# One block of convolution and recurrence: four banks for the first DFT stage, other steps for recurrence, filter network and final preparation

## The chip, the cores and the metric

The kernel runs on one core of one Trainium2 chip. The core has a matrix engine (TensorE, PE in the profile; PEld is its weight load), a vector engine (VectorE, DVE), a scalar engine (ScalarE, ACT), a general engine (GpSimd, POOL), and SyncE (SP), which here only issues DMAs. The metric is device time in microseconds (us) of one execution; lower is better. A matmul's result goes to PSUM, which has eight banks of 128 x 512 fp32 values; DVE or ACT must read a bank ("evacuate" it) before PE writes it again.

## What is computed

A block for 4096 latent tokens and 256 context tokens of 1024 values: a modulated RMS norm, one input projection, a gated long convolution (Hyena) on one part of the columns, a recurrence in both directions (RG-LRU) on the other, and one output projection onto the residual.

```python
def hyena_filter(L, f_w1, ..., f_freq):          # 2L x 512, from a small network
    z = jnp.concatenate([t, jnp.cos(f * w), -jnp.sin(f * w)], axis=-1)
    h = jnp.sin(fr[0] * (z @ f_w1 + f_b1))
    h = jnp.sin(fr[1] * (h @ f_w2 + f_b2))
    h = jnp.sin(fr[2] * (h @ f_w3 + f_b3))
    h = (h @ f_w4) * jnp.exp(-t * deltas[None, :])
    ...
def long_conv(u, kernel, bias):
    uf = jnp.fft.rfft(u, n=2 * L, axis=1)
    kf = jnp.fft.rfft(kernel, n=2 * L, axis=0)
    y = jnp.fft.irfft(uf * kf[None], n=2 * L, axis=1)[:, :L]
    return y + u * bias
def rglru_bidir(xr, ...):                        # gates a, b from two small products
    xc = dwconv(xr, conv_w, (2, 1)) + conv_b
    hf = linear_scan(a_f, b_f, h0_f, False)      # h = a * h + b along the tokens
    hb = linear_scan(a_b, b_b, h0_b, True)       # the same from the last token back
def mixer_out(p, y_rnn, kernel, ...):
    u = dwconv(p[..., :3 * D_HYENA], hy_conv_w, (1, 1)) + hy_conv_b
    x0, x1, v = jnp.split(u, 3, axis=-1)
    y_h = long_conv(v * x1, kernel, hy_bias) * x0
    y = jnp.concatenate([rms_norm(y_h, gn_h) * silu(z_h), rms_norm(y_rnn, gn_r) * silu(z_r)], axis=-1)
    return y @ w_out
```

## The kernel before

Every fp32 product of the two projections is made of three fp16 products (high by high, high by low, low by high), so an output tile of 128 x 512 takes 24 matmuls. The long convolution is a DFT of 8192 points split into 128 x 64, in fp16 pairs too. The program has these stages; the times are those of the profiled execution.

- **Start (0 to 62 us).** The modulation products `mod` (tile `wm` streams in), the first four token tiles are loaded and normed (`xsplit`, L454: scale on DVE; L456: high fp16 half on ACT; L458: low half on POOL; L459/L460: two DMA transposes on SP into `X`), and the weights of the `xr` columns are prepared (tile `wh`).
- **Pass A (62 to about 850 us).** Eight chunks of 512 tokens, twelve steps each; a step is one output tile of `xr`, `x1` or `v` (24 matmuls `mm<-X,wh`). Side work is hung on a step list: `at(d, f)` calls `f` d steps later, `tick()` runs what is due. The side work of the first chunk or two is the weights, the context (`ctx_in` at step CT = 5, 7, 9; its gates are `fa<-xc,gw` and ACT L788), and the filter network `mlp`: three layers by four pieces of 512 positions, a matmul pair (a fp32 matmul is two instructions) into `fa` or `fb`, one ACT pass, five DVE passes (L850 to L854: `q`, `q`, `x`, `x`, `x`) and a sine on ACT (L855) each. At step FS = 10 `filt` begins the filter itself: 16 groups of rows (`filter_group`), a new one about every FD = 4.95 steps.
- **Pass B (about 850 to 1790 us).** Chunks 7 to 0, twelve steps each (`zr`, `x0`, `zh`). The backward recurrence `units_b` is a generator of seven phases: loads; gates; their exponentials; square root; scan with the product into `zr` and its sum of squares; `yscale`, which puts that sum through PE (`p2b_yr`, a matmul into `sm`) to find a scale; the scaled fp16 halves to DRAM. The steps at which chunks 7 to 1 advance it are in DS; chunk 0 has its own (D0).
- Beside pass B `fft_gen` advances, 1.75 pulls a step: the first DFT stage of u (`s1u_gen`, 64 groups, about 925 to 1222 us), then the per-slot work, then the inverse.
- **Phase out (about 1852 to 2241 us).** 32 output tiles of 128 tokens, four per chunk: `ohalf` with `wz,hl` (24 matmuls x 2) for the convolution's half, and with `X,hl` for the recurrence's, seven to eight tiles ahead. `oprep` prepares the next chunk's `hl` in three parts, called after the tiles OP1, OP2 and OP3 of a chunk; the third part writes `hl` (L1430 on ACT, L1431 on DVE).

A scheduler sorts each engine's instructions by priority, which the code's order gives; matmuls made with `mms` rank 64 places lower. PSUM is shared by all: `mm` 3 banks, `fa` 2, `fb` 2, `sm` 1. One group of the first DFT stage is

```python
vo = pool.tile([128, 4, 2, 128], F16, name="vo", bufs=2)
ps = self.pst("fa", 2)
self.mms(ps, st1[:, 0:128], rhs, True, False)
self.mms(ps, st1[:, 128:256], rhs, False, True)
nc.scalar.activation(vo[:, :, 0, :], pv, AF.Copy)             # L1160
nc.vector.tensor_sub(vo[:, :, 1, :], pv, vo[:, :, 0, :])      # L1161
nc.sync.dma_start(self.VuD[:, j, n0:n0 + 4, :], ...)          # L1163
```

and four groups share one transposed input `ut`, which comes from `ua` (L1148 ACT, L1149 DVE) by a DMA transpose.

Of the kernel before, what the change touches and what calls it, by code (L numbers as in the profile page):

```python
# [10 lines left out]
F32 = mybir.dt.float32  # L11
F16 = mybir.dt.float16
# [10 lines left out]
D = 1024  # L23
# [6 lines left out]
CT = 5  # L30
ML = 1
MK = 1
FS = 10
RQ = 1
OD = 7
OP1 = (0, 0)
RL = 8
IZ = 3
OP2 = 1
OP3 = 2  # L40
PW = ()
IA = (1, 1)
FL = (2, 3)
# [4 lines left out]
MS = ()  # L48
XS = ((1, 1, 2), (1, 2, 3))
PB = {"mm": 3, "fa": 2, "fb": 2, "sm": 1}  # L50
FD = 4.95
XK = ((6, 9), (0, 4))
NX = 11
D0 = (8, 11, 12, 13, 14, 16, 17, 17)
WO = (9, 13, 16)
SEQ = [(2, "zr"), (2, "x0"), (1, "x0"), (1, "zr"), (0, "x0"), (0, "zh"), (0, "zr"), (2, "zh"), (1, "zh")]
XL = [(6, "zr"), (5, "zr"), (4, "zr"), (3, "zr"), (2, "zr"), (1, "x0"), (0, "x0"), (2, "zh")]
DS = (1, 4, 7, 7, 9, 9, 10)
DA = ((12, 14, 15, 15), (4, 4, 6, 6), (3, 5, 6, 8))
EPS = 1e-6  # L60
MAGIC = 1.5 * 2.0 ** 23
# [102 lines left out]
class K:  # L164
# [420 lines left out]
    def pass_a(self):  # L585
        tc, nc, a = self.tc, self.nc, self.a
        with ExitStack() as es, ExitStack() as right:
# [9 lines left out]
            ml = ml_.__enter__()  # L597
            sp_ = tc.tile_pool(name="start", bufs=1)
            sp = sp_.__enter__()
            if True:  # L600
                self.columns(sp)
                self.tap_sums()
                m = self.mod(sp, ml, ap, 1)
                next(m)
                self.cpos = ap.tile([128, 512], F32, name="cpos")
                for h in range(2):
                    nc.scalar.dma_start(self.cpos[64 * h:64 * h + 64], a["t_pos"])
                xt = [hy.tile([128, 1028], F32, name="xc", bufs=4)[:, :D] for k in range(3)]
                xr = [self.xload(ap, tok(0), 0, xt[:2], xt[2].rearrange("p (k c) -> p k c", k=2)),
                      self.xload(ap, tok(2), 2)]  # L610
                raw = self.xp_.tile([128, NB, 8, 128], F32, name="X", bufs=2)
                for j in range(NB):
                    nc.sync.dma_start(raw[:, j], a["w_in"][COLS["xr"] + j])
                self.pull(m)
                m = self.mod(sp, ml, ap, 0)
                next(m)
                for k in range(2):
                    self.xsplit(ap, xr[k], self.s1, self.sx, dst(X, 2 * k))
                gs = [self.wprep("xr", j, raw[:, j]) for j in range(NB)]
                for k in range(2):  # L620
                    for j, g in enumerate(gs):
                        W["xr", j] = next(g)
                self.pull(m)
                for g in gs:
                    next(g)

            def wpair(k):
                raw = sp.tile([128, 2, 8, 128], F32, name="wm", bufs=4)
# [13 lines left out]
            def filt():  # L642
# [4 lines left out]
                next(g)  # L647
                for d in FL:
                    self.at(d, lambda: next(g))
            mlp = self.mlp(ml)  # L650
            for k in range(4):
                self.at(k, lambda k=k: wpair(NB + 2 * k))
            self.at(3, recur)
# [2 lines left out]
            ctx = self.ctx_in(ap, hy, W)  # L656
            for d in (0, 2, 4):
                self.at(CT + d, lambda: next(ctx))
            for k in range(10):
                self.at(ML + k // MK, lambda: self.pull(mlp, 1))  # L660
            self.at(FS, filt)
            for n in range(16):
                self.at(FS + FG + int(FD * n), lambda n=n: self.filter_group(self.flt, n))
# [165 lines left out]

    def mlp(self, pool):  # L830
        nc, a = self.nc, self.a
        ws = pool.tile([128, D], F32, name="bm", bufs=1)[:, :384].rearrange("p (l c) -> p l c", l=3)
        nc.scalar.dma_start(ws, a["f_w"])
        fc = pool.tile([128, 6], F32, name="fc")
        nc.vector.tensor_mul(fc[:, 0:3], self.col[:, 104:107], self.col[:, 107:110])
# [299 lines left out]
    def s1u_gen(self, pool, st1):  # L1135

        nc = self.nc
        for j in range(NB):
            u = pool.tile([128, T], F32, name="u", bufs=1)
            for h in range(2):  # L1140
                nc.sync.dma_start(u[:, 2048 * h:2048 * h + 2048], self.uD[j][:, 2048 * h:2048 * h + 2048])
            tot = self.cp.tile([128, 1], F32, name=f"ut{j}")
            nc.vector.tensor_reduce(tot, self.usq[:, j], axis=AX.X, op=OP.add)
            s, self.su[j] = self.pow2(self.cp, tot, 9, 0, f"u{j}", 1)
            uv = u.rearrange("c (m n) -> c n m", n=64)
            for q in range(4):
                ua = pool.tile([128, 16, 2, 64], F16, name="ua", bufs=1)
                nc.scalar.activation(ua[:, :, 0, :], uv[:, 16 * q:16 * q + 16, :], AF.Copy, scale=s)  # L1148
                nc.vector.scalar_tensor_tensor(ua[:, :, 1, :], uv[:, 16 * q:16 * q + 16, :], s, ua[:, :, 0, :],  # L1149
                                               op0=OP.mult, op1=OP.subtract)  # L1150
                ut = pool.tile([128, 16, 128], F16, name="ut", bufs=2)
                nc.sync.dma_start_transpose(ut, ua.rearrange("c n h m -> c (n h m)"))
                for g in range(4):
                    vo = pool.tile([128, 4, 2, 128], F16, name="vo", bufs=2)
                    ps = self.pst("fa", 2)
                    rhs = ut[:, 4 * g:4 * g + 4, :]
                    self.mms(ps, st1[:, 0:128], rhs, True, False)
                    self.mms(ps, st1[:, 128:256], rhs, False, True)
                    pv = ps.rearrange("p (n c) -> p n c", c=128)
                    nc.scalar.activation(vo[:, :, 0, :], pv, AF.Copy)  # L1160
                    nc.vector.tensor_sub(vo[:, :, 1, :], pv, vo[:, :, 0, :])  # L1161
                    n0 = 16 * q + 4 * g
                    nc.sync.dma_start(self.VuD[:, j, n0:n0 + 4, :], vo.rearrange("p n h c -> p n (h c)"))  # L1163
                    yield
# [356 lines left out]
```

## Time and profile before

| what | value |
|---|---|
| median of 3 runs | 2239.83 us (2232.47 to 2243.2) |
| profiled execution | 2242.97 us |
| its span in the trace | 2241.2 us |
| PE busy | 1934.0 us, 86% of the span |
| DVE, ACT, POOL busy | 1362.1, 1173.0, 623.2 us |
| mean granted clock of PE | 0.943 of full speed |

The profiled execution lies 3.1 us above the median, inside the range of the runs, and 1.8 us above its span. PE has the largest busy share in every stage; what it idles is 2241.2 - 1934.0 = 307 us. A row of a timeline gives in brackets how long the engine was idle before it and whose work ended that.

### The profile page before, as it was taken

To read this page: it belongs to the slowest core of one execution; us is meant where nothing else is said; L and a number is where in the kernel's file an instruction comes from. 1 tells how busy PE (TensorE), PEld (TensorE's weight loads), DVE (VectorE), ACT (ScalarE), POOL (GpSimd) and SP (SyncE) were. 2 spreads that over 40 slices of the span, in tenths; PEclk is the share of its full clock that TensorE was granted. 3 is DMA by queue.
4 is the path that set the end of the run, shared out by engine and by line. 5 is a ranking of instruction groups with operands and counts; after the bars stand their busy time and mean duration, and the time that the engine had idled before them with its cause. 6 is when DMAs were issued, how large, how long until landed. Compare 5 with 4: busy or idle time off the path is not lost. (4 is left out here: it accounts for less than half of the span.)

```text
span 2241.2 us, 30015 instructions
## 1 busy us (share of the span) xinstructions
PE 1934.0 (86%) x10640; PEld 933.0 (42%) x10640; DVE 1362.1 (61%) x2629; ACT 1173.0 (52%) x1828; POOL 623.2 (28%) x417
## 2 busy tenths in 40 slices
PE   6866989989889899878888989898898858999997
PEld 2443434434334344333334545454443434444443
DVE  3894676756647567564543663744745565766576
ACT  2655766664656578576573733744556531432232
POOL 3024344343424321111211342533423300111130
PEclk9987989999999999989999999999999879999999
DMA  9547354565544522666746889889998798344332
GB/s 286 196 123 209 102 184 136 179 171 150 191 126 129 141 90 84 204 184 196 219 147 212 200 202 253 216 217 232 236 234 229 186 264 234 112 143 150 115 125 104
DMA packets 397028, 398.43 MB, mean 178 GB/s; under 512 B 208809, under 2 KB 295359, under 8 KB 392270
## 3 DMA queue, kind: packets, MB, share of 16 engines
q1 hardware_dynamic: 381020, 356.93, 56.4%
q10 hardware_dynamic: 15858, 39.59, 6.0%
q8 instruction: 84, 1.38, 0.3%
q14 instruction: 66, 0.54, 0.1%
HBM read 206.62 MB, written 146.81 MB: 158 GB/s over the span
## 5 line engine op out<-in xcount | busy, mean ns | idle before, releaser
L169 PE MATMUL mm<-X,wh 128*128 128x512 f16 x3072 | 733.4, 386 | 32.2 <-DVE cvx L536 10.2
L169 PEld LDWEIGHTS <-wh 128*128 128x128 f16 x3648 | 325.8, 100 | 455.5 <-issue 93.4
L169 PE MATMUL mm<-X,wz 128*128 128x512 f16 x1536 | 371.9, 389 | 9.8 <-ACT zh L1023 5.0
L169 PEld LDWEIGHTS <-wz 128*128 128x128 f16 x1728 | 158.2, 100 | 226.7 <-issue 58.8
L169 PEld LDWEIGHTS <-hl 128*128 128x128 f16 x1536 | 149.7, 99 | 222.7 <-issue 37.8
L169 PE MATMUL mm<-wz,hl 128*128 128x512 f16 x768 | 176.7, 385 | 18.4 <-DVE oxt L1445 6.9
L169 PE MATMUL mm<-X,hl 128*128 128x512 f16 x768 | 174.7, 382 | 9.5 <-DMA hl<-hlD 9.5
L463 POOL TENSOR_TENSOR acc<-acc,dec 128x512 f32<-128x512 f32 x64 | 88.1, 1377 | 237.2 <-ACT dec L941 227.7
L463 POOL TENSOR_TENSOR oacc<-oacc,osq 128x512 f32<-128x512 f32 x21 | 38.5, 1833 | 330.9 <-ACT oacc L1417 327.8
L466 POOL TENSOR_TENSOR I<-I,xc 128x1024 f32<-128x1024 f32 (+3 forms) x36 | 84.4, 2348 | 161.4 <-ACT I L788 155.0
L169 PE MATMUL fa<-xc,gw 128*128 128x512 f32 (+3 forms) x152 | 79.2, 614 | 46.2 <-DVE cvv L531 19.4
L1201 POOL TENSOR_TENSOR A<-A,B 128x256 f32<-128x256 f32 x64 | 53.1, 829 | 229.1 <-DVE B L1200 194.9
L458 POOL TENSOR_TENSOR xlo<-xt,xh 128x1024 f16<-128x1024 f32 x32 | 74.3, 2344 | 140.1 <-ACT xh L456 140.1
L169 PE MATMUL fb<-tb,vki 128*128 128x128 f16 x768 | 98.2, 225 | 14.6 <-DMA tb<-in_t_s 9.8
L169 PE MATMUL fa<-tb,vu 128*128 128x128 f16 x768 | 97.7, 225 | 0.0
L812 DVE TENSOR_TENSOR_SCAN I<-R,car,I 128x512 f32<-128x512 f32 (+2 forms) x64 | 97.2, 1540 | 0.1
L1212 DVE SCALAR_TENSOR_TENSOR yy<-A,yy 128x512 f16<-128x512 f32 x64 | 56.6, 885 | 64.6 <-ACT yy L1211 64.5
L1199 DVE TENSOR_TENSOR A<-fa,kf 128x512 f32<-128x512 f32 x64 | 43.9, 686 | 81.0 <-ACT kf L1195 78.1
L169 PEld LDWEIGHTS <-vki 128*128 128x128 f16 x768 | 77.2, 101 | 29.5 <-issue 17.9
L466 POOL TENSOR_TENSOR zr<-zr,sg 128x1024 f32<-128x1024 f32 x16 | 39.5, 2466 | 175.7 <-ACT sg L1069 140.9
L169 PE MATMUL fb<-xc,gw 128*128 128x512 f32 (+3 forms) x152 | 77.8, 601 | 10.2 <-ACT I L788 5.0
L463 POOL TENSOR_TENSOR hf<-hf,I 128x1024 f32<-128x1024 f32 x16 | 50.0, 3127 | 129.1 <-DVE I L812 82.2
(345 smaller groups left out, 3420.8 us busy)
## 6 DMA issues: line engine op xcount, KB each, us to landing
VkD<-vk SPq DMA_DIRECT2D x64, 256.0 KB, 2.4
VuD<-vo SPq DMA_DIRECT2D x64, 256.0 KB, 2.6
X<-XD SPq DMA_DIRECT2D x8, 2048.0 KB, 9.6
vu<-VuD SPq DMA_DIRECT2D x128, 128.0 KB, 3.7
vki<-VkD SPq DMA_DIRECT2D x128, 128.0 KB, 3.3
ZD<-zo SPq DMA_DIRECT2D x64, 256.0 KB, 3.5
xt<-in_x SPq DMA_DIRECT2D x30, 512.0 KB, 5.0
xpD<-xt SPq DMA_DIRECT2D x28, 512.0 KB, 3.7
```

The source lines that it names most:

```text
L169: self.nc.tensor.matmul(out, lhsT, rhs, start=start, stop=stop)
L458: nc.gpsimd.tensor_sub(xl, xt, xh)
L463: self.nc.gpsimd.tensor_add(out, x, y)
L466: self.nc.gpsimd.tensor_mul(out, x, y)
L812: nc.vector.tensor_tensor_scan(f(h), f(r), f(h), 0.0 if c is None else c, op0=OP.mult, op1=OP.add)
L1199: nc.vector.tensor_mul(A, u4, kf[:, :, 0:1, :].to_broadcast([128, NB, 2, 64]))
L1201: nc.gpsimd.tensor_sub(A[:, :, 0, :], A[:, :, 0, :], B[:, :, 1, :])
L1212: nc.vector.scalar_tensor_tensor(yy[:, :, 1, :], yv, 0.125, yy[:, :, 0, :], op0=OP.mult, op1=OP.subtract)
```

## The change

There are four edits. The first DFT stage of u takes its PSUM banks in turn from `fb` and `fa` (four in all, where it had the two `fa`), with four output tiles `vo` and two input tiles `ua`. The steps DS of the backward recurrence become (1, 4, 6, 7, 8, 10, 11): exponentials and scan a step earlier, the scale and the fp16 halves a step or two later. OP2 and OP3 become 0 and 1, so the second and third part of `oprep` are called one output tile earlier. The filter network leaves the step list: it has a weight tile of its own, its first part is called in the start behind the weight loads, five more parts behind the second modulation's first part, and the rest at the end of the start; `filt` comes at step 5, its groups every 5.2 steps.

```diff
-FS = 10
+FS = 5
...
-OP2 = 1
-OP3 = 2
+OP2 = 0
+OP3 = 1
...
-FD = 4.95
+FD = 5.2
...
-DS = (1, 4, 7, 7, 9, 9, 10)
+DS = (1, 4, 6, 7, 8, 10, 11)
...
                 for j in range(NB):
                     nc.sync.dma_start(raw[:, j], a["w_in"][COLS["xr"] + j])
+                mlp = self.mlp(ml)
+                self.pull(mlp, 1)
                 self.pull(m)
                 m = self.mod(sp, ml, ap, 0)
                 next(m)
+                self.pull(mlp, 5)
                 for k in range(2):
                     self.xsplit(ap, xr[k], self.s1, self.sx, dst(X, 2 * k))
...
                 for g in gs:
                     next(g)
+                self.pull(mlp)
...
-            mlp = self.mlp(ml)
...
-            for k in range(10):
-                self.at(ML + k // MK, lambda: self.pull(mlp, 1))
...
-        ws = pool.tile([128, D], F32, name="bm", bufs=1)[:, :384].rearrange("p (l c) -> p l c", l=3)
+        ws = pool.tile([128, 3, 128], F32, name="ws")
...
-                ua = pool.tile([128, 16, 2, 64], F16, name="ua", bufs=1)
+                ua = pool.tile([128, 16, 2, 64], F16, name="ua", bufs=2)
...
-                    vo = pool.tile([128, 4, 2, 128], F16, name="vo", bufs=2)
-                    ps = self.pst("fa", 2)
+                    vo = pool.tile([128, 4, 2, 128], F16, name="vo", bufs=4)
+                    ps = self.pst("fa" if g % 2 else "fb", 2)
```

How the order of instructions moves is shown at three places. First DVE in the start, where the first four token tiles are scaled (`xc` and `xt`, L454). Before:

```order
L315 SCALAR_TENSOR_TENSOR rq_x<-rt_x,rq_x 128x2 x2
L295 TENSOR_SCALAR sw<-col,es 128x4
L454 SCALAR_TENSOR_TENSOR xc<-xc,rq_x,s_149 128x1024 x2
L454 SCALAR_TENSOR_TENSOR xt<-xt,rq_x,s_149 128x1024 x2
L489 SCALAR_TENSOR_TENSOR wh<-X,p2s_w,wh 128x1024
```

After the change (`q` and `x` are the filter network's tiles):

```order
L454 SCALAR_TENSOR_TENSOR xc<-xc,rq_x,s_149 128x1024
L851 TENSOR_SCALAR q<-x 128x512 x2
L852 TENSOR_SCALAR q<-q 128x512 x2
L853 SCALAR_TENSOR_TENSOR x<-q,x 128x512 x2
L854 SCALAR_TENSOR_TENSOR x<-q,x 128x512 x2
L855 TENSOR_SCALAR x<-x 128x512 x2
L454 SCALAR_TENSOR_TENSOR xc<-xc,rq_x,s_149 128x1024
L315 SCALAR_TENSOR_TENSOR rq_x<-rt_x,rq_x 128x2
L358 TENSOR_TENSOR mr<-mm,bm 2x256
L454 SCALAR_TENSOR_TENSOR xt<-xt,rq_x,s_149 128x1024
L863 TENSOR_TENSOR q<-x,q 128x512
L454 SCALAR_TENSOR_TENSOR xt<-xt,rq_x,s_149 128x1024
```

Ten passes of the filter network now stand between the first two scalings, and twenty more stand ahead of the first; eight of its twelve matmul pairs stand ahead of the first matmul of `X` on PE. On SP six loads of `w_in` now stand ahead of the last pair of transposes of `X`, two of them ahead of the first pair and three more ahead of the second; before it was one, ahead of the third pair.

The second place is PE at the first groups of the first DFT stage of u (`st1u` are its constants, `ut` its input). Before:

```order
L169 LDWEIGHTS st1u
L169 MATMUL fa<-ut,st1u 128x512
L169 LDWEIGHTS st1u
L169 MATMUL fa<-ut,st1u 128x512
L169 LDWEIGHTS st1u
L169 MATMUL fa<-ut,st1u 128x512
L169 LDWEIGHTS st1u
L169 MATMUL fa<-ut,st1u 128x512
L169 LDWEIGHTS wh
L169 MATMUL mm<-X,wh 128x512
```

After:

```order
L169 LDWEIGHTS st1u
L169 MATMUL fb<-ut,st1u 128x512
L169 LDWEIGHTS st1u
L169 MATMUL fb<-ut,st1u 128x512
L169 LDWEIGHTS st1u
L169 MATMUL fa<-ut,st1u 128x512
L169 LDWEIGHTS st1u
L169 MATMUL fa<-ut,st1u 128x512
L169 LDWEIGHTS st1u
L169 MATMUL fb<-ut,st1u 128x512
```

Where two groups stood together ahead of the projection's matmuls, four now do, in four banks.

The third place is DVE at the end of chunk 7's backward recurrence (`q1r` and `p2b_yr` lead to the scale's matmul on PE). Before:

```order
L1087 TENSOR_TENSOR zr<-zr,hf 128x1024
L1161 TENSOR_TENSOR vo<-fa,vo 128x4x128
L814 COPY car_8311<-I 128x1
L1087 TENSOR_TENSOR zr<-zr,hf 128x1024
L1149 SCALAR_TENSOR_TENSOR ua<-u,p2s_u_8373,ua 128x16x64
L1111 TENSOR_REDUCE q1r<-qs 128x1
L190 CAST p2b_yr<-q1r 128x1
```

After:

```order
L1088 TENSOR_TENSOR zr<-zr,hf 128x1024
L815 COPY car_8276<-I 128x1
L1088 TENSOR_TENSOR zr<-zr,hf 128x1024
L1162 TENSOR_TENSOR vo<-fb,vo 128x4x128
L1162 TENSOR_TENSOR vo<-fa,vo 128x4x128
L1150 SCALAR_TENSOR_TENSOR ua<-u,p2s_u_8341,ua 128x16x64 x2
L1112 TENSOR_REDUCE q1r<-qs 128x1
L190 CAST p2b_yr<-q1r 128x1
```

One more `ua` pass and two `vo` passes stand ahead of `p2b_yr`. On PE the number of projection matmuls (`mm`) between the chunk's last gate matmul and the `p2b_yr` matmul goes, for chunks 7, 6, 5, 4, 3, 2, 1, 0, from 73, 107, 100, 121, 70, 66, 85, 90 to 103, 127, 127, 152, 74, 67, 89, 101.

## Rows read from the trace of the kernel before

**Rows 1.** Page part 1: busy time, share of the span, instructions.

```profile
PE 1934.0 (86%) x10640; PEld 933.0 (42%) x10640; DVE 1362.1 (61%) x2629; ACT 1173.0 (52%) x1828; POOL 623.2 (28%) x417
```

**Rows 2.** Windows: us, busy time per engine (instructions), PE clock, DMA share, GB/s.

```profile
0.00:62.00 62.00, 38.54 (x148) 13.86 (x149) 26.93 (x93) 20.56 (x30) 20.62 (x16) 0.89 1.00 281
...
118.00:213.00 95.00, 60.20 (x359) 36.71 (x358) 63.28 (x168) 48.84 (x96) 32.98 (x20) 0.83 0.60 144
213.00:850.00 637.00, 577.04 (x2407) 253.15 (x2408) 423.68 (x771) 403.68 (x678) 243.51 (x149) 0.96 0.48 149
850.00:1240.00 390.00, 339.16 (x1699) 154.91 (x1698) 204.38 (x364) 242.47 (x331) 76.42 (x35) 0.95 0.59 179
...
1880.00:2241.20 361.20, 326.93 (x1684) 151.69 (x1681) 230.87 (x488) 100.38 (x155) 48.45 (x29) 0.98 0.39 127
```

**Rows 3.** Waits, 118 to 213 us: total, times, longest.

```profile
PE mm L169 <- DMA X<-xh: 8.9, 1, 8.9
...
PE mm L169 <- DVE xc L536: 7.1, 1, 7.1
...
PE fa L169 <- ACT R L788: 6.5, 1, 6.5
...
PE fb L169 <- ACT x L855: 4.4, 2, 2.3
ACT L788 <- DMA dec<-in_f_w: 4.0, 1, 4.0
```

**Rows 4.** Timeline of PE in pass A: start, length, count, idle before it.

```profile
83.63 1.02 PE L169 MATMUL fb<-x,bm 66*128 66x512 f32 x2
...
123.72 10.52 PE L169 MATMUL mm<-X,wz 128*128 128x512 f16 x48
```

**Rows 5.** Timeline of DVE at the start.

```profile
42.29 4.35 DVE L454 SCALAR_TENSOR_TENSOR xt<-xt,rq_x,s 128x1024 f32<-128x1024 f32 x2
```

**Rows 6.** Tile x on DVE (MLP): ns min/median/max, first and last start.

```profile
L850 DVE TENSOR_SCALAR q<-x x12: 410/418/427, 85.5 to 157.8; 128x512 f32<-128x512 f32 x12
...
L853 DVE SCALAR_TENSOR_TENSOR x<-q,x x12: 681/683/2487, 88.8 to 160.6; 128x512 f32<-128x512 f32 x12
```

**Rows 7.** Timeline of POOL, 130 to 142 us.

```profile
134.89 6.42 POOL L458 TENSOR_TENSOR xlo<-xt,xh 128x1024 f16<-128x1024 f32 x2 [76.14 <-ACT xh L456]
```

**Rows 8.** Timeline of DVE, 130 to 142 us.

```profile
136.84 2.49 DVE L853 SCALAR_TENSOR_TENSOR x<-q,x 128x512 f32<-128x512 f32 x1
```

**Rows 9.** Timeline of SP's DMA queue at the start.

```profile
56.70 1.79 SPq L460 DMA_TRANSPOSE X<-xlo  x1
```

**Rows 10.** Waits, 850 to 1240 us.

```profile
DVE vo L1161 <- ACT vo L1160: 49.6, 22, 7.7
...
ACT vo L1160 <- DMA VuD<-vo: 23.0, 10, 5.5
...
PE fa L169 <- DVE vo L1161: 21.3, 12, 5.3
...
PE sm L169 <- DVE p2b_yr L190: 7.1, 1, 7.1
```

**Rows 11.** Tile vo: ns min/median/max, first and last start.

```profile
L1160 ACT ACTIVATE vo<-fa x64: 572/590/630, 936.7 to 1220.8; 128x512 f16<-128x512 f32 x64
L1161 DVE TENSOR_TENSOR vo<-fa,vo x64: 664/690/705, 938.9 to 1221.5; 128x512 f16<-128x512 f32 x64
```

**Rows 12.** Waits, whole span.

```profile
PE sm L169 <- DVE p2b_yr L190: 28.8, 5, 9.4
```

**Rows 13.** Waits, 1880 to 2241 us.

```profile
PE mm L169 <- DVE oxt L1445: 6.9, 4, 2.0
...
PE mm L169 <- DVE hl L1431: 4.7, 8, 0.7
...
PE mm L169 <- ACT hl L1430: 3.3, 2, 1.8
```

**Rows 14.** Timeline of PE in the middle of pass A.

```profile
566.60 2.08 PE L169 MATMUL fa<-xc,gw 128*128 128x512 f32 x2 [8.33 <-DVE cvv L531]
```

## The prediction

> **What bounds the kernel now.** I read the page's busy times first: PE works 1934.0 of 2241.2 us, DVE 1362.1, the others less [rows 1]. So only PE's idle time, 307 us, can be won unless PE's own work or its clock changes; the edits add no matmul. The windows say where that idle time lies: 23.5 us of the first 62 (62.00 - 38.54), 34.8 of the 95 from 118 to 213, 60 of the 637 of pass A after that, 51 of the 390 in which the first DFT stage of u runs, 34 of the last 361 [rows 2]. The start is not held by an engine: its DMA share is 1.00. From 118 to 213 us PE is idle for more than a third of the time and its granted clock is 0.83, against 0.96 in the next window [rows 2]; that is the stretch of the filter network and the context.
>
> Then I read, stage by stage, which wait of PE ends last. From 118 to 213 us: 4.4 us for the network's sine, 7.1 for `xc`, 6.5 for the context's first gate, 8.9 for the next `X` behind it [rows 3]. In the first DFT stage: 21.3 us in 12 waits for `vo`, and 7.1 for chunk 7's `p2b_yr` [rows 10]. Over the span `p2b_yr` costs 28.8 us in five waits, the longest, 9.4, in chunk 0 [rows 12]. In phase out: 4.7 us for DVE's `hl`, 3.3 for ACT's, 6.9 for the evacuation into `oxt` [rows 13]. These names are the ones that the edits touch, and they sum to some 92 us. In pass A's middle there are stalls of about 8 us, of which one is shown [rows 14]; they end on DVE's convolution passes, which wait for ACT, and the filter's rows share ACT and POOL with them.
>
> The durations are those of the profiled execution, 2242.97 us (span 2241.2, 1.8 around it), 3.1 above the median of 2239.83. The sum is made against 2242.97.
>
> **Start and filter network.** The network is twelve pieces. One takes a pair of matmul instructions, 1.02 us [rows 4], and five DVE passes: three of 0.42 and two of 0.68 (the short ones taken alike), 2.62 us [rows 6]. Nothing is removed; it is moved.
>
> Gain: eight of the twelve pairs come to stand ahead of the first `X` matmul, where PE is idle anyway. 8 x 1.02 is 8.2; since the record's end includes the pipeline I take 0.86 a pair, -7. The waits of 4.4 for the sine go for those eight, but four pieces remain in chunk 0: -3.
>
> Cost: 30 DVE passes, six pieces, stand ahead of the fourth `xt` scaling: 6 x 2.62 = 15.7, and with one more pass about 16.4 us, if all were in line. DVE is busy only 26.93 us of the first 62 [rows 2], and 20 of the 30 passes stand ahead of the first scaling, in that idle time; ten stand between the first two. The first two scalings take 4.35 us a pair in these rows [rows 5], two passes of about 2.2. I take a delay of 5 us for the first `X` matmuls: the ten passes are 5.2. The ends are 0 (all in idle time) and 16.4.
>
> One row speaks against putting DVE's passes beside POOL: the pass that takes 0.68 in the median took 2.49 at 136.84 us [rows 6, 8], within POOL's two subtractions, 6.42 us from 134.89 [rows 7]. POOL is busy 20.62 us in the first 62 [rows 2]. If each of its microseconds held DVE up, the ten or thirty passes would be late by up to 20.6; by the rows, one such meeting costs 1.8 us. My 5 us includes that two or three of the passes meet no POOL work. The Trainium skill, "SBUF — State Buffer", section "SBUF: two separate sides", says that DVE and GpSimd share a port pair as an exclusive lock, so that a DVE operation with two SBUF inputs and a GpSimd operation that reads SBUF shut each other out for a whole instruction. The trace agrees in that one case of 2.49 us; by the rule the start would pay once for each meeting, which is the slower rival's mechanism below.
>
> On SP, five `w_in` loads move ahead of transposes. A transpose's time in that queue was 1.79 us [rows 9]; five transfers at that price are 9 us at most, and 0 if the transposes wait longer for `xh` and `xlo` anyway. I take 0, since DMA must move these bytes before 62 us or right after in either order.
>
> Then the context. Its gate waited for ACT, which waited 4.0 for the filter's constants `dec` [rows 3]; these loads now stand some 40 ACT rows earlier. The 6.5 and 8.9 are one stall in two parts, since `X` comes late behind the same queues. `filt` at step 5 also puts filter rows, matmuls that wait for none of this, into the stretch. I take -9 of 15.4, and -4 of the 7.1 for `xc`, since ACT and DVE no longer have the network's passes there. The ends are 0 and all of it. Sum of this part: +5 - 7 - 3 - 9 - 4 = -18; ends +46 (the slower rival, below) and -34 (-7 - 4.4 - 7.1 - 15.4, start free).
>
> **First DFT stage.** ACT's pass takes 0.59 us and DVE's 0.69 [rows 11], so a bank is held for 1.28 us beyond its matmul even when nothing queues. With two banks the third of four groups of one `ut` waits for the first; with four, no group of a `ut` waits for its own bank, only for those of the `ut` before, several projection steps back. The 23.0 us that ACT waits for `VuD<-vo` [rows 10] is the wait for one of two `vo` buffers, and it delays the bank's release: four buffers remove it. What remains is that DVE waits 49.6 us for ACT's half [rows 10], which neither banks nor buffers shorten: the engines' own queues. If these are late by more than four groups, the wait returns. I take two thirds of 21.3, -14; ends -4 and -21. A longer `fb` use delays nobody here: the gates take `fb` and `fa` in turn, which I cost at nothing, and at a quarter of the gain if they meet (inside the ends).
>
> **Recurrence steps.** What counts is how much independent PE work stands between the last gate matmul and the `p2b_yr` matmul. Per matmul 10.52 / 48 = 0.219 us [rows 4]. Chunk 7 gets 30 more, 6.6 us against a wait of 7.1 [rows 10], but one more `ua` pass stands ahead of it on DVE, about 2.2 us by the scaling pass of the same size [rows 5]: -4.4. The other four waits are 28.8 - 7.1 = 21.7 [rows 12], all in late chunks, where the order gains only 4, 1, 4 and 11 matmuls: 20 x 0.219 = 4.4. Sum -9. Chunks 6, 5 and 4 gain 20 to 31 matmuls but have no such wait to lose. Ends -2 (chunk 7's DVE queue absorbs its share) and -19 (28.8 less chunk 0's 9.4). The scaled halves are written a step later and read only in phase out: nothing.
>
> **Final preparation.** `hl` is made one tile, 48 matmuls or 10.5 us, earlier. DVE's 4.7 us are within that, and go. Of ACT's 3.3 a part falls on the last chunks and I count 1.5. The 6.9 for `oxt` are waits for evacuations; `hl`'s DVE passes only move to other evacuations, so they stay. -6; ends -2 and -15.
>
> **Filter groups** in pass A's middle: same work at other steps. The stalls there [rows 14] are two engines' queue phases, which a shift by five steps can make or break: 0, ends -15 and +15, two such stalls of about 8.
>
> **Sum.** -18 - 14 - 9 - 6 + 0 = -47: 2242.97 - 47 = 2196, and 3 less on the scale of the median, 2193. I say 2195.
>
> **Rivals.**
> (1) *The waits only move on.* For it: DVE's 49.6 us for ACT's half, and that late chunks gain few matmuls. Then the start gives +5 - 7 - 3 = -5, the DFT stage -4, the steps -2, the preparation -2: -13, 2230.
> (2) *No change.* As (1), and the filter's new phase adds two stalls of 8 us: +15, 2245. For it: the 8 us stall exists already [rows 14] and nothing in the diff cares for it; against: a new phase can as well remove one.
> (3) *Slower, by the start alone.* The network's passes stand in line with the scaling (16.4), POOL and DVE hold each other up (20.6), and the five loads delay the transposes (9): +46. With the later stages' -29 that is +17, 2260. It decides once the start loses more than 40 us (29 and the 11 of half a per cent). Against: DVE is idle 35 us there, and twenty passes stand in it.
> (4) *All of it goes.* -34 - 21 - 19 - 15 = -89; and with fewer gaps from 118 to 213 us the clock there may rise from 0.83 to 0.96, worth 60.2 x (1 - 0.83 / 0.96) = 8 on its own. 2243 - 97 = 2146. For it: the edits name just the releasers of these waits.
>
> **How the numbers follow.** The forecast, 0.53, with its own range 2170 to 2215 (halves of the unsure terms either way); (1) 0.2; (2) 0.1; (3) 0.07; (4) 0.1. Half a per cent, about what a measurement of this kernel can tell from none, is 11 us: 2229 to 2251. Rival (1) lies on that bound, half to each side. Faster: 0.53 + 0.1 + 0.1 = 0.73. Same: 0.1 + 0.08 of (2) = 0.18. Slower: 0.07 + 0.02 of (2) = 0.09. The range leaves out (3), (2) and part of (4): 2160 to 2232.
>
> **What would show it.** First `X` matmul about 67 us instead of 62; PE's idle time from 118 to 213 us below 25 instead of 34.8, with no wait on the sine of 2 us; waits of PE for `vo` under 8 us in the DFT stage, and ACT's for `VuD<-vo` near nothing; chunk 7's `p2b_yr` wait near 3, those of chunks 3 to 0 hardly smaller; `hl` waits by DVE near nothing in phase out. The prediction is wrong if the first `X` matmul comes after 80 us, if DVE or ACT, not the banks, turn out to release the DFT groups, or if pass A's middle has more or fewer stalls of 8 us than before.

## The result, and the profile after

The changed kernel took 2180.16 us in the median of 4 runs (2176.79 to 2183.24); the kernel before, run beside it, 2236.15 (2231.22 to 2243.2). The ratio is 0.975, 95% interval 0.9721 to 0.9779: 56 us faster. The forecast was 2195 within 2160 to 2232, so sign and range held. The parts of the sum did not all hold, and the experiments below say which.

The profiled execution of the changed kernel has a span of 2176.4 us, 65 less than that of before; the one of before lies 6.8 us above its median of 2236.15 and that of the changed kernel 2.0 below its own, so differences between the two traces overstate by about 9 us.

The page's busy times, which answer to [rows 1]:

```profile
PE 1917.2 (88%) x10640; PEld 931.7 (43%) x10640; DVE 1363.7 (63%) x2629; ACT 1170.2 (54%) x1827; POOL 609.2 (28%) x417
```

PE's idle time fell from 307 to 2176.4 - 1917.2 = 259 us, 48 less, and its busy time by 17, with the same 10640 instructions and the same mean granted clock (0.943). Why the same instructions were busy 17 us less was not taken apart. The windows of the changed kernel at the stages, with the columns of [rows 2]; the last three are the middle of pass A, the first DFT stage and phase out, at their places in this trace:

```profile
0.00:62.00 62.00, 46.77 (x155) 16.10 (x156) 34.93 (x102) 24.77 (x39) 13.40 (x14) 0.92 0.96 293
62.00:118.00 56.00, 41.30 (x343) 20.37 (x343) 47.49 (x150) 32.42 (x53) 6.94 (x3) 0.83 0.67 190
118.00:213.00 95.00, 76.99 (x529) 45.17 (x528) 60.88 (x178) 54.54 (x107) 38.02 (x26) 0.88 0.58 156
305.00:806.00 501.00, 460.13 (x1912) 204.28 (x1911) 337.50 (x597) 310.11 (x525) 196.85 (x120) 0.96 0.52 157
898.00:1196.00 298.00, 258.32 (x1165) 115.86 (x1164) 152.56 (x243) 183.79 (x244) 61.90 (x27) 0.93 0.67 198
1808.00:2176.40 368.40, 350.23 (x1800) 164.61 (x1798) 245.34 (x504) 108.69 (x165) 42.58 (x29) 0.97 0.45 145
```

The kernel before, from 62 to 118 us and at the same three places:

```profile
62.00:118.00 56.00, 53.77 (x483) 26.66 (x484) 47.23 (x155) 35.51 (x57) 0.00 (x0) 0.97 0.51 182
...
311.00:825.00 514.00, 461.17 (x1893) 203.03 (x1891) 336.49 (x598) 314.58 (x533) 198.20 (x122) 0.96 0.50 153
917.00:1230.00 313.00, 265.27 (x1168) 117.16 (x1167) 157.34 (x245) 187.48 (x246) 62.74 (x27) 0.94 0.63 191
1852.00:2241.20 389.20, 354.57 (x1800) 163.75 (x1800) 244.65 (x505) 108.41 (x165) 48.45 (x29) 0.97 0.43 138
```

Windows at fixed times compare different work once one kernel runs ahead. So I counted projection matmuls (`mm<-X,wh` and `mm<-X,wz`, 4608 in each trace) on PE and read the time at which the next one starts after a given count. 432 is the middle of chunk 1, and 2304 all of pass A; by this count pass A ends near 890 us in the kernel before, not at about 850. This table is worked out that way, in us; the other columns are the first projection matmul, the first matmul of the first DFT stage (`st1u`), the end of its last one, the first matmul on `hl`, and the span's end.

| kernel | first | count 432, chunk 1 | 2304, end of pass A | DFT stage, first | DFT stage, last | first `hl` matmul | end |
|---|---|---|---|---|---|---|---|
| before | 62.0 | 255.0 | 889.6 | 933.7 | 1220.8 | 1852.4 | 2241.2 |
| changed | 76.5 | 248.9 | 871.7 | 913.8 | 1188.7 | 1807.6 | 2176.4 |
| difference | +15 | -6 | -18 | -20 | -32 | -45 | -65 |

So the start loses 15 us, the context wins 21, the rest of pass A 12, the way to the DFT stage 2, the first DFT stage 12, the rest of pass B 13 and phase out 20. A second trace of the changed kernel, of a run 9 us longer, has differences of +16, -4, -15, -16, -29, -41 and -55: a single trace settles a stage to some 6 us.

The start, in the timelines of PE, DVE and ACT of the changed kernel (three fences):

```profile
76.54 0.59 PE L169 MATMUL mm<-X,wh 128*128 128x512 f16 x1 [10.31 <-DMA X<-xh]
```
```profile
50.20 1.28 DVE L454 SCALAR_TENSOR_TENSOR xc<-xc,rq_x,s 128x1024 f32<-128x1024 f32 x1
...
52.74 3.21 DVE L853 SCALAR_TENSOR_TENSOR x<-q,x 128x512 f32<-128x512 f32 x2
...
57.76 1.27 DVE L454 SCALAR_TENSOR_TENSOR xc<-xc,rq_x,s 128x1024 f32<-128x1024 f32 x1
```
```profile
68.10 0.63 ACT L862 ACTIVATE q<-x 128x512 f16<-128x512 f32 x1 [6.01 <-DMA hD<-q]
68.64 1.04 ACT L456 ACTIVATE xh<-xt 128x1024 f16<-128x1024 f32 x1
```

The first scaling starts at 50.2 us. Before, the first two began at 39.90 and those of `xt`, the third and fourth tile, at 42.29 [rows 5]:

```profile
39.90 2.48 DVE L454 SCALAR_TENSOR_TENSOR xc<-xc,rq_x,s 128x1024 f32<-128x1024 f32 x2
```

In the changed kernel the second scaling follows 7.6 us after the first, with the ten network passes between. The fourth split's ACT pass then stands behind one of the network's, which waited 6.0 us for its table writes to leave the buffer.

Part of the lateness is older than the scaling. A modulation product (`mm<-mr,ident`) leads, through `s`, to the norm's factor `sxf`, and on PE the network's first pairs now stand ahead of it. Rows of PE and DVE, before and then changed:

```profile
31.03 0.69 PE L169 MATMUL mm<-mr,ident 2*128 2x256 f32 x2 [1.68 <-DVE mr L360]
...
37.23 0.34 DVE L399 TENSOR_SCALAR sxf<-p2r_sx 128x1 f32<-128x1 f32 x2
```
```profile
25.77 2.05 PE L169 MATMUL fb<-x,ws 66*128 66x512 f32 x2 [3.63 <-DMA x<-in_t_z]
...
39.19 0.69 PE L169 MATMUL mm<-mr,ident 2*128 2x256 f32 x2
...
42.00 0.33 DVE L399 TENSOR_SCALAR sxf<-p2r_sx 128x1 f32<-128x1 f32 x2
```

The product is 8.2 us later and the factor 4.8. So of the 10.3 us by which the first scaling is late, 4.8 come to DVE from upstream and 5.5 arise in its own line. The loss of 15 us is close to the 16.4 that the prediction gave for "all in line", but partly by luck, since the delay upstream is no part of that term.

### The profile page after: what moved, and what is told of

Same layout as the page of the kernel before. It is cut to its first block, busy times and chain, and to the rows that moved or that the text cites. A ratio compares the mean times of both kernels' runs of the same rounds, so it can differ in the third digit from the quotient of the medians.

```text
span 2176.4 us, 29975 instructions
## 1 busy us (share of the span) xinstructions
PE 1917.2 (88%) x10640; PEld 931.7 (43%) x10640; DVE 1363.7 (63%) x2629; ACT 1170.2 (54%) x1827; POOL 609.2 (28%) x417
## 5 line engine op out<-in xcount | busy, mean ns | idle before, releaser
L169 PE MATMUL mm<-X,wz 128*128 128x512 f16 x1536 | 367.1, 386 | 4.8 <-DVE cva L555 3.4
L466 POOL TENSOR_TENSOR I<-I,xc 128x1024 f32<-128x1024 f32 (+3 forms) x36 | 82.8, 2304 | 195.9 <-ACT I L789 172.5
L463 POOL TENSOR_TENSOR oacc<-oacc,osq 128x512 f32<-128x512 f32 x21 | 32.6, 1552 | 301.8 <-ACT oacc L1418 298.8
L805 DVE SCALAR_TENSOR_TENSOR xc<-xh,xc 128x1024 f32<-128x1024 f32 (+2 forms) x34 | 49.0, 1440 | 68.2 <-ACT xh L802 58.7
```

The source lines that it names most:

```text
L169: self.nc.tensor.matmul(out, lhsT, rhs, start=start, stop=stop)
L463: self.nc.gpsimd.tensor_add(out, x, y)
L466: self.nc.gpsimd.tensor_mul(out, x, y)
L805: nc.vector.scalar_tensor_tensor(Z, M, 1.0, Z, op0=OP.add, op1=OP.mult)
```

## The experiments

Every kernel was timed beside the kernel before; "-12" means that the median was 12 us below the median of the kernel before in the same job (2233.5 to 2233.9).

| kernel | median us | ratio | 95% interval | against before |
|---|---|---|---|---|
| banks and buffers alone | 2221.61 | 0.9946 | 0.9926 to 0.9967 | -12 |
| steps alone | 2234.06 | 1.0004 | 0.9990 to 1.0019 | 0 |
| preparation alone | 2213.61 | 0.9907 | 0.9890 to 0.9924 | -20 |
| network and filter alone | 2213.62 | 0.9912 | 0.9894 to 0.9930 | -20 |
| changed, old steps | 2185.54 | 0.9786 | 0.9762 to 0.9810 | -48 |
| network alone, filter as before | 2227.93 | 0.9973 | 0.9961 to 0.9985 | -6 |
| buffers alone, two banks | 2224.46 | 0.9950 | 0.9931 to 0.9969 | -9 |
| changed, splits first | 2188.41 | 0.9791 | 0.9772 to 0.9811 | -45 |
| changed, again | 2176.65 | 0.9747 | 0.9723 to 0.9771 | -57 |
| changed, network split in two | 2186.38 | 0.9797 | 0.9771 to 0.9823 | -47 |
| last part of preparation alone | 2212.07 | 0.9900 | 0.9877 to 0.9922 | -22 |
| changed, groups 4.95 apart | 2191.07 | 0.9811 | 0.9789 to 0.9833 | -43 |

The four edits one by one sum to -12.3 + 0.1 - 20.3 - 20.3 = -52.8, against -56 together.

### The four edits one by one

**Banks and buffers alone.** The kernel before with

```diff
-                ua = pool.tile([128, 16, 2, 64], F16, name="ua", bufs=1)
+                ua = pool.tile([128, 16, 2, 64], F16, name="ua", bufs=2)
-                    vo = pool.tile([128, 4, 2, 128], F16, name="vo", bufs=2)
-                    ps = self.pst("fa", 2)
+                    vo = pool.tile([128, 4, 2, 128], F16, name="vo", bufs=4)
+                    ps = self.pst("fa" if g % 2 else "fb", 2)
```

Expected: 

> The kernel before with the four banks, four vo and two ua alone. Theory (the banks were what the first DFT groups waited for): PE's wait for vo falls from 21.3 us to under 6 and the time by 12 to 16 us, as the changed kernel's trace gains about 14 between chunk 7 and chunk 5. Rival (the evacuating engines set the pace, the wait only moves on): less than 5 us faster, with new waits on the gates or on the recurrence's scale in that stretch of the same size as those that went.

Measured: 12 us faster. The waits from 850 to 1240 us of this kernel:

```profile
PE sm L169 <- DVE p2b_yr L190: 19.4, 2, 10.4
...
PE fb L169 <- ACT I L788: 7.8, 3, 4.8
...
ACT vo L1160 <- DMA VuD<-vo: 2.6, 2, 2.4
```

PE's wait for `vo`, 21.3 us before [rows 10], is no longer among its waits. But part of it turned up elsewhere: the scale's matmul waits 19.4 us in two chunks where it was 7.1 in one [rows 10], the gates 7.8 where they were 3.6 in the same window before:

```profile
PE fb L169 <- ACT I L788: 3.6, 2, 2.7
```

From the stage's first to its last matmul it is 287.1 us before and 271.9 here; PE's idle time in between falls by 9, from 44.9 to 35.5 us, and its busy time by 6. The theory holds in its total; the rival's mechanism is there too and takes over half of the 21.3.

**Steps alone.** The kernel before with the new DS line.

```diff
-DS = (1, 4, 7, 7, 9, 9, 10)
+DS = (1, 4, 6, 7, 8, 10, 11)
```

Expected: 

> The kernel before with the new steps of the backward recurrence alone. Theory of the prediction: 9 us faster, half in chunk 7 (wait 7.1 to about 3) and half in the late chunks. Rival, after the changed kernel's trace: chunk 7's wait does not shrink (it was 10.5 us there), the late chunks' waits (2.9, 3.9, 5.5, 9.4) shrink to a few us, and the time falls by 3 to 8 us.

Measured: no difference (1.0004, up to 0.2% either way). In its trace chunk 7's wait for the scale is still 7.1 us, and those of the late chunks are gone except for one of 3.7. In their place PE's timeline between 1695 and 1790 us shows the inverse DFT's matmuls waiting for their loads and for DVE:

```profile
1702.28 0.21 PE L169 MATMUL fa<-dn,oz 128*128 128x64 f16 x1 [8.72 <-DMA oz<-ZD]
...
1719.05 0.87 PE L169 MATMUL fa<-dn,wr 128*128 128x64 f16 x24 [3.36 <-DMA wr<-ZD]
...
1768.75 0.21 PE L169 MATMUL fa<-dn,oz 128*128 128x64 f16 x1 [5.91 <-DVE Y L1272]
```

These 18 us stand against the 14.9 of chunks 1 and 0 (5.5 and 9.4) that went. Both expectations fell: the waits for the scale can go and the time stay.

**Preparation alone.** The kernel before with OP2 and OP3 one tile earlier.

```diff
-OP2 = 1
-OP3 = 2
+OP2 = 0
+OP3 = 1
```

Expected: 

> The kernel before with the final preparation's parts called one tile earlier alone. Theory (hl was late at every chunk's end, and the wait for oxt behind it was the same stall): about 20 us faster, all of it behind 1880 us, the six waits of about 2 us for oxt or wh gone together with the waits for hl. Rival of the prediction: only the hl waits go, 6 us. Second rival: phase out is shorter in the changed kernel for a reason upstream, so less than 5 us here.

Measured: 20 us faster, as the theory said, three times what the prediction gave.

**Network and filter alone.** The kernel before with `mlp` in the start and the filter's new steps.

```diff
-FS = 10
+FS = 5
...
-FD = 4.95
+FD = 5.2
...
+                mlp = self.mlp(ml)
+                self.pull(mlp, 1)
...
+                self.pull(mlp, 5)
...
+                self.pull(mlp)
...
-                self.at(ML + k // MK, lambda: self.pull(mlp, 1))
...
```

Expected: 

> The kernel before with the filter network ahead of chunk 0 and the filter at step 5, every 5.2 steps, alone. Theory: first X matmul 14 us later, 20 us won back by the middle of chunk 1, and another 13 over chunks 2 to 8 from the filter's new phase: 17 to 22 us faster in all. Rival: the gain over chunks 2 to 8 is not from this edit, so 5 to 8 us faster.

Measured: 20 us faster. In its trace the first `X` matmul comes at 78 us, count 432 at 246 and count 2304 at 871, which is the changed kernel's course through pass A (77, 249 and 872).

### What within the edits did it

**Network alone.** The same edit without its first four changed lines: the network moved, FS = 10 and FD = 4.95 kept.

```diff
 FS = 10
...
 FD = 4.95
...
+                self.pull(mlp, 1)
...
+                self.pull(mlp, 5)
...
```

Expected: 

> The kernel before with the filter network moved, but the filter still from step 10, every 4.95 steps. Theory (the network's move wins the start and the context, the filter's phase wins chunks 2 to 8): some 7 us faster, all of it by chunk 1, and the 8 us stalls of pass A's middle as before. Rival (the phase brings nothing of itself; the network's move frees ACT and DVE): about 20 us faster, as with the phase.

Measured: 6 us faster, and in its trace the lead of 8 us at count 432 is 4 at count 2304. So of the 20 us some 14 come from the filter's own steps.

**Groups 4.95 apart.** The changed kernel with one line put back.

```diff
-FD = 5.2
+FD = 4.95
```

Expected: 

> The changed kernel with the filter's groups 4.95 steps apart again, still from step 5. Theory (where a group's rows meet the gates of a chunk decides; five steps earlier is a shift of nearly a whole group, so only the spacing changed the meeting): some 10 us slower than the changed kernel, with three or four stalls of 8 us or more in pass A's middle. Rival (the earlier start alone brings it, since the filter's tail leaves the last chunk): within 3 us of the changed kernel.

Measured: 14 us slower than the changed kernel run beside it (0.9811 against 0.9747, the intervals apart). So with the filter from step 5 it is the spacing that brings the gain. A spacing of 5.2 from step 10 was not run, so whether the earlier start is needed for it is not shown. Its window over pass A's middle, to be read against those of before and after above:

```profile
307.00:830.00 523.00, 470.10 (x1911) 206.22 (x1910) 337.12 (x606) 312.89 (x530) 199.32 (x122) 0.95 0.49 150
```

PE idles 53 us here, as before (53), and 41 with 5.2. But these windows start behind a stall of 12.1 us that the changed kernel has at 280 us, where this one has 8.2 and the kernel before 3.3. Between the counts 432 and 2304, with that stall, the stretch takes 634.6 us before, 631.4 here and 622.8 in the changed kernel, and PE idles 60.7, 62.0 and 55.6. So of the 12 us between before and changed some 5 are idle time and 7 are PE's busy time, of which a part is work that now lies ahead of count 432 (2475 instructions of PE in the stretch instead of 2495).

The gates do not explain the gain. Two of their stalls are, in this kernel,

```profile
469.64 2.08 PE L169 MATMUL fa<-xc,gw 128*128 128x512 f32 x2 [9.43 <-ACT R L789]
...
662.08 2.08 PE L169 MATMUL fa<-xc,gw 128*128 128x512 f32 x2 [8.73 <-DVE cvv L531]
```

and in the changed kernel the first of the two, while the second is 7.4:

```profile
463.64 2.07 PE L169 MATMUL fa<-xc,gw 128*128 128x512 f32 x2 [5.00 <-DVE kd L939]
```

But others grew, the one at 280 and one at 560 (9.6 us, where it is 7.6 here), and all gate matmuls of the stretch together wait 41.0 us before, 43.4 here and 41.3 in the changed kernel. Which filter row meets which pass in each chunk was not taken apart, so why 5.2 is better than 4.95 stays open.

**Last part of the preparation alone.** The kernel before with one line.

```diff
-OP3 = 2
+OP3 = 1
```

Expected: 

> The kernel before with the last part of the final preparation alone one tile earlier (the middle part stays). Theory (the hl passes of DVE at a chunk's last tile held the evacuations of oxt and wh, so that 15 us of waits and not only hl's hang on the third part): 16 to 20 us faster. Rival (both parts are needed, since the third waits for the second's totals): under 8 us faster.

Measured: 22 us faster, as much as both parts. The waits of PE's `mm` matmuls in its phase out, all that there are:

```profile
PE mm L169 <- DMA hl<-hlD: 10.5, 1, 10.5
...
PE mm L169 <- ACT hl L1430: 1.8, 1, 1.8
...
PE mm L169 <- DVE hl L1431: 0.3, 1, 0.3
```

The 6.9 us for `oxt` and the 3.6 for `wh` went with the 4.7 for `hl` [rows 13]; the 3.6 is this row of the kernel before:

```profile
PE mm L169 <- DVE wh L1445: 3.6, 2, 2.2
```

They were one stall, and its second half ends on a load. In the kernel before, DVE's `hl` passes at a chunk's last tile hold back PE and also the final norm of a finished tile (L1460, then L1464), which stands behind them on DVE. Only when that tile is stored is the next residual loaded into it (L1390), and some 13 us behind the `hl` wait the evacuation (L1445) waits for this load, and PE for the evacuation. One such chunk, on DVE, in ACT's DMA queue and on PE:

```profile
1994.97 3.49 DVE L1431 SCALAR_TENSOR_TENSOR hl<-oz,p2s_yh,hl 128x1024 f16<-128x1024 f32 x2
1998.38 1.23 DVE L1460 TENSOR_SCALAR os<-os 128x2 f32<-128x2 f32 x1
...
2002.90 2.48 DVE L1464 SCALAR_TENSOR_TENSOR wh<-wh,rq_f,fg 128x1024 f32<-128x1024 f32 x2
...
2010.49 1.41 DVE L1445 SCALAR_TENSOR_TENSOR wh<-mm,rrr,wh 128x512 f32<-128x512 f32 x2 [2.04 <-DMA wh<-xpD]
```
```profile
2006.89 0.33 ACTq L1390 DMA_DIRECT2D wh<-xpD  x1
```
```profile
1998.51 3.63 PE L169 MATMUL mm<-wz,hl 128*128 128x512 f16 x16 [0.74 <-DVE hl L1431]
...
2011.30 2.75 PE L169 MATMUL mm<-wz,hl 128*128 128x512 f16 x12 [1.39 <-DVE wh L1445]
```

Six chunks show this pair of waits. With the third part a tile earlier an evacuation still waits some 2 us for its load, but PE no longer waits for it. The chain is read from the trace; no run here moves the norm alone.

**Buffers alone.** The kernel before with four `vo` and two `ua`, in the two `fa` banks.

```diff
-                ua = pool.tile([128, 16, 2, 64], F16, name="ua", bufs=1)
+                ua = pool.tile([128, 16, 2, 64], F16, name="ua", bufs=2)
-                    vo = pool.tile([128, 4, 2, 128], F16, name="vo", bufs=2)
+                    vo = pool.tile([128, 4, 2, 128], F16, name="vo", bufs=4)
```

Expected: 

> The kernel before with four vo and two ua tiles, but the first DFT stage still in the two fa banks. Theory (the banks decide): ACT's wait for VuD<-vo goes, PE's for vo stays at 15 us or more, less than 4 us faster. Rival (the vo buffers held the banks): PE's wait for vo under 8 us and 10 to 12 us faster, nearly all that the four banks gave.

Measured: 9 us faster; the intervals of this and of banks and buffers together cover each other. Its waits from 850 to 1240 us:

```profile
PE fa L169 <- DVE vo L1161: 17.1, 7, 7.7
...
PE sm L169 <- DVE p2b_yr L190: 8.8, 1, 8.8
...
ACT ua L1148 <- DMA ut<-ua: 7.2, 4, 2.7
...
ACT vo L1160 <- DMA VuD<-vo: 0.6, 1, 0.6
```

PE's wait for `vo` falls only from 21.3 to 17.1, as the theory said, and still most of the time is won, as the rival said: neither was right. From the stage's first to its last matmul it is 274.3 us, and PE idles 36.1 of them, nearly the same as with four banks (271.9 and 35.5). ACT's wait for `VuD<-vo` went, 23.0 us before [rows 10], and its wait for `ut<-ua` halved, in the same window before

```profile
ACT ua L1148 <- DMA ut<-ua: 15.1, 9, 3.9
```

By the medians the two banks more bring 3 us on top of the buffers, which is within the noise. The banks without the buffers were not run, nor `vo` and `ua` one by one.

**Changed, old steps, and changed, again.** The changed kernel with the old DS line, and, in another job, the changed kernel unaltered.

```diff
-DS = (1, 4, 6, 7, 8, 10, 11)
+DS = (1, 4, 7, 7, 9, 9, 10)
```

Expected: 

> The changed kernel with the recurrence steps DS put back. Theory (the wait only moves on to the inverse DFT's loads, as the steps alone gave nothing): the same time as the changed kernel, within 5 us, 2180 to 2185. Rival (the steps need the four banks to bring their 9 us): 8 to 10 us slower than the changed kernel, 2188 to 2190, with waits on the scale's matmul of 9 us in chunk 6 and in chunk 0 again, as in the kernel with the banks alone.

Expected: 

> The changed kernel again, beside the others of this job. Both theories: 2178 to 2183 us, 0.975 of the kernel before; if it lies within 3 us of the run with the old steps (2185.5 at a ratio of 0.9786), the steps bring nothing beside the banks either, if 5 us or more below it they do.

Measured: 2185.5 with the old steps; the changed kernel 2176.7 here and 2180.2 the first time. By the medians the steps bring 5 to 9 us beside the other edits. The two intervals (0.9762 to 0.9810 and 0.9723 to 0.9771) overlap by a little, so this is likely and not settled. The traces agree with it: the wait of the scale's matmul over the whole span is, with the old steps and then in the changed kernel,

```profile
PE sm L169 <- DVE p2b_yr L190: 39.2, 6, 10.4
```
```profile
PE sm L169 <- DVE p2b_yr L190: 14.3, 3, 10.5
```

and chunk 6's, which the banks had made, is in the kernel with the old steps

```profile
1065.94 0.16 PE L169 MATMUL sm<-p2b_yr,onesb 128*128 128x1 bf16 x1 [7.56 <-DVE p2b_yr L190]
```

where PE's idle time is 0.16 us in the changed kernel. So the steps take back what the DFT stage's edit turned into a new wait.

### Two tries to mend the start

**Splits first.** The changed kernel with the five parts of the network behind the token splits.

```diff
-                self.pull(mlp, 5)
                 for k in range(2):
                     self.xsplit(ap, xr[k], self.s1, self.sx, dst(X, 2 * k))
+                self.pull(mlp, 5)
```

Expected: 

> The changed kernel with the five parts of the filter network called behind the four token splits instead of ahead of them. Theory (DVE's passes in line ahead of the scaling and ACT's wait for the network's table writes ahead of the last split made the first X matmul 14.6 us late): first X matmul at 62 to 67 us instead of 76.5, and half of that or more kept to the end: 5 to 10 us faster than the changed kernel. Rival (chunk 0 waits for the network and the context anyway, which then come later by as much): same time as the changed kernel, the gain gone by chunk 1.

Measured: 2188.4, 8 to 12 us slower than the changed kernel by the medians. The last transpose of `X` starts at 65 us instead of 72, but the first `X` matmul still comes at 77:

```profile
76.95 0.82 PE L169 MATMUL mm<-X,wh 128*128 128x512 f16 x3
```

PE was working from 65.9 us on, at network pairs and modulation products that stand ahead of it in its order. And what was put behind falls into chunk 0, which ends later (count 432 at 261 us instead of 249).

**Network split in two.** The changed kernel with two parts ahead of the splits and three behind.

```diff
-                self.pull(mlp, 5)
+                self.pull(mlp, 2)
                 for k in range(2):
                     self.xsplit(ap, xr[k], self.s1, self.sx, dst(X, 2 * k))
+                self.pull(mlp, 3)
```

Expected: 

> The changed kernel with two of the five parts of the filter network ahead of the token splits (the rest of the first half's layers) and three behind (its table writes and the second half's first layer). Theory (ACT's 6 us wait for the table writes and ten DVE passes between the splits make the first X matmul late): first X matmul at 65 to 70 us instead of 76.5, and 3 to 8 us faster than the changed kernel. Rival (the lateness is made good by the end of the context anyway, or the moved parts fall into chunk 0, as when all five were put behind): same or up to 8 us slower.

Measured: 2186.4, 10 us slower than the changed kernel run beside it, though the intervals touch. ACT no longer waits for the table writes ahead of the fourth split, and the first `X` matmul is still at 77 us:

```profile
77.02 3.60 PE L169 MATMUL mm<-X,wh 128*128 128x512 f16 x8 [7.73 <-DMA X<-xh]
```

The first scaling starts at 51.5 us, late already, behind the first half's network passes. So my cause for the late start, the six-microsecond wait, was not what set it; taking it out moved nothing. What both tries leave as it was is the network's first part, ahead of the modulation product: that product runs at 39.9 us in both, 39.2 in the changed kernel and 31.0 before. A kernel with this part behind the product was not run, so what it costs at the first `X` matmul stays open. No version here beat the changed kernel.

## Why the prediction was right in the sum and wrong in its parts

The sum was -47 and the time fell by 56, within the likeliest case's range. That is in part luck: the start gave 12 us less than its term, the filter groups and the final preparation some 14 more each. Two of the prediction's own signs of being wrong came true: the buffers, not the banks, gave most of the DFT stage's gain, and from count 432 to 2304 the changed kernel has two stalls of 8 us or more (9.6 the smaller) where the kernel before has four (8.1 to 9.6). Part by part:

- **Start and filter network, -18.** Mis-sized: the network alone gives -6. The delay of the first `X` matmul was taken as 5 us and was 15. Two premises failed. The network's pairs were to stand "where PE is idle anyway"; the first of them stand ahead of the modulation product, and the factor `sxf` comes at 42.0 us instead of 37.2. And the passes that I had put into DVE's idle time stood in line: ten run between that factor and the first scaling at 50.2, and ten more before the second at 57.8. The gain behind it was some 21 us to the middle of chunk 1, where I had counted 23: with waits on the sine gone from 118 to 213 us, and 18 us idle there instead of 34.8 [rows 2]. In that stretch DVE, not PE, had the larger busy time before (63.28 us against 60.20 [rows 2]), so the statement that PE leads in every stage does not hold there. The fourth rival's clock of 0.96 did not come: the granted clock rose from 0.83 to 0.88 there, and from 62 to 118 us, where PE was busy 41.30 us instead of 53.77, it fell from 0.97 to 0.83.
- **The lock of DVE and GpSimd**, weighed there: two L853 passes took 3.21 us instead of 1.37 beside POOL's subtraction, one meeting at the 1.8 us of [rows 6, 7]. And the 4.35 us in [rows 5], read as the price of the first two scalings, are those of the second two, which ran beside POOL's subtractions; the first two took 2.48, and the last two in the changed kernel 1.26 and 1.27. Beside the last of these it was POOL's subtraction, begun 0.07 us later, that took longer (3.52 us instead of 2.15). So this is a cost of some 2 us that the kernel before had too, and not the 20 of the slower rival. POOL before, and changed:

```profile
42.41 6.22 POOL L458 TENSOR_TENSOR xlo<-xc,xh 128x1024 f16<-128x1024 f32 x2 [7.87 <-ACT xh L456]
```
```profile
52.66 2.15 POOL L458 TENSOR_TENSOR xlo<-xc,xh 128x1024 f16<-128x1024 f32 x1 [17.55 <-ACT xh L456]
61.22 3.52 POOL L458 TENSOR_TENSOR xlo<-xc,xh 128x1024 f16<-128x1024 f32 x1 [6.41 <-ACT xh L456]
```

- **Filter groups, 0.** Wrong: about -14, by two comparisons (network and filter against network alone, and 5.2 against 4.95 steps). I had the stalls [rows 14] and their names but put the shift at nothing, within 15 either way; the bound held it. How the spacing brings it is not shown.
- **First DFT stage, -14.** -12: right in size. Its reason was half right. The wait for `vo` went with four banks, but the buffers alone won 9 of the 12 and left most of that wait. The step that failed is "two thirds of 21.3" as a saving of its own: a named wait of PE went whole, and over half of it came back at the gates and the scale. The Trainium skill, "Perfetto Trace Analysis", section "Matmuls", says that independent matmul groups should rotate through different PSUM banks so that one's evacuation overlaps the next one's matmuls; by the runs here, the buffers behind the evacuation were worth 9 us, and rotation through two banks more another 3, within the noise.
- **Recurrence steps, -9.** Alone 0, beside the others -5 to -9. Chunk 7's wait did not shrink to 3; it is 10.5 us. The late chunks' waits went, further than the count of matmuls said, and became waits for the inverse DFT's loads. What the steps did bring lies in chunk 6, where the kernel before has no such wait at all: the prediction said that chunks 6 to 4 had none to lose, which the banks and buffers changed.
- **Final preparation, -6.** Mis-sized: -20 to -22. The step that failed is "`hl`'s DVE passes only move to other evacuations, so they stay", of the 6.9 us for `oxt`. They went, with the 3.6 for `wh`; by the trace before, the evacuations were late through the final norm that stood behind those passes. The far end of 15 was short as well: in the trace of the last part alone phase out is 21.5 us shorter, 17.3 of it idle time of PE and 4.2 busy time of the same 1800 instructions.

Of the rivals, the first (waits only move on) describes the steps alone and half of the banks' wait. The second (two stalls more) did not come, and the fourth (all of it goes, -89) is too large, though for the final preparation its 15 was too small. The slower one had part of its mechanism at work in the start (15 us of its 46): the passes in line came, the five loads' 9 us did not, since the second pair of transposes left at 61.2 us, right behind its `xh` (60.1 to 61.1). Its consequence did not come, because the context had more to win.

## What to carry to other kernels

Where a short wait for a producer repeats at a fixed place in a loop and a second wait, for evacuations, follows it, count both: calling the producer one tile earlier took away 20 us where the first wait showed only 5. Follow the second wait back past the evacuation: here it ended on a load whose buffer came free late. A wait's row is not what its removal is worth: here it was about half of the row in the DFT stage, nothing for the steps alone, and four times the row in phase out. The next dependent step (here the scale's matmul, then the inverse DFT's loads) stands ready to take the rest, and moving that step too can win some of it back. Where side work is hung on a fixed spacing beside a loop of fixed length, try a few spacings: 5.2 against 4.95 steps was worth 14 us here.

## What the runs showed that was not expected

A network pair put into PE's idle time in the start was not free: the modulation product behind it on PE, and with it the norm's factor, came 8.2 and 4.8 us later. In phase out a producer's two passes on DVE cost PE more through the store and load of another tile than through the producer's own result. A stage's idle time can be nearly the same (36.1 and 35.5 us) with a PE wait of 17 us on one tile and with none of it.
